# A four-layer hybrid trunk: more buffers for the local kernel blocks of the second S5 layer, and a third product buffer in the first

## The chip, the cores and the metric

The kernel runs on one core of one Trainium2 chip. The metric is the device time of one execution in microseconds (us). A lower time is better. Three executions of the kernel before were timed.

## What is computed

The reference passes 128 context tokens and 256 latent tokens (384 columns in all, 1024 features) through four residual layers: an S5 layer, a retention layer, a Hyena layer, and a second S5 layer. Only the S5 layers bear on the change. Cut to what matters:

```
u, gate = split(h @ w_in)
for d in (forward, backward):
    state[t] = A * state[t-1] + B u[t]      # 64 groups, 64 complex states each
    y       += Re(C state)
y = gelu(y)                                  # y includes d_skip * u
y = y * sigmoid(y @ w_glu + b_glu)
out = (y * silu(gate)) @ w_out
```

All data is 32-bit floating point. A dense product is made three times, with each operand split into a high part (hi) and the rest (lo).

## The kernel before, in words

The S5 scan is done in chunks of 8 tokens, 48 chunks. Within a chunk, the outputs come from a Toeplitz matrix of the local kernel. Across chunks, only the states at the chunk ends are stepped, 32 steps long, in `recur` (L771), on DVE, in two halves of 32 groups: `R0` and `R1` in the plans (L809). Each step takes a product, a shuffle and two sums (L793 to L796), and the steps of the two halves stand interleaved in DVE's order.

The stage around the change is the output stage of an S5 layer, in `s5` (L699). Channels go in 8 blocks, two at a time: four pairs, the loop over `m` (L860).

- `toeplitz(m)` (L845) loads the local kernel of block m from the scratch array `kd`: 8 transfers of 64 KB on the SP queue (L850) into one tile `Tt`. TensorE transposes it in 8 pieces into two PSUM tiles (L855), and ScalarE copies each into a half tile `Tm` (L856). `Tt` has 2 buffers, `Tm` has 7 (`TMH`). Blocks 0 to 3 are written ahead of the loop (`TMB` = 4), and block m+4 after the products of pair m (L883).
- `CP` holds the output matrices of the states, four tiles for a pair. In the second S5 layer they are loaded on the POOL queue (L867). In the first, 6 of the 16 are loaded and 10 are made by `gen_c` (L684): for each of two directions DVE writes one product into `CP` (L629) and a second product into a tile `xt` (L630), and a transfer issued by POOL adds `xt` to `CP` (L632). `xt` has 2 buffers there, and is free again when the transfer has landed.
- The products of a pair (L882) add three terms in PSUM: `Tm` by the input, and the forward and backward states by `CP`. There are 96 of them for a pair, 48 for each half r. Pairs 0 and 1 (m = 0, 2) read states of the half that R0 steps, pairs 2 and 3 (m = 4, 6) those of R1.
- Then ScalarE copies the sums (L888), TensorE transposes them (L894), and ScalarE and DVE make the GELU (L900 to L903), which also sets the PSUM tile free.

PSUM tiles of this stage (`psm`) have 4 buffers. The weight slabs `wr` (1 MB each, L153) share the SP queue with the kernel blocks, and have 2 buffers. Among them in this stage are slabs of `s5_w_in`, then four of `mod_w` (L838, read by TensorE at L379), then `s5_w_glu`. A weight is split by a cast on ScalarE (L162) and a subtraction on POOL (L134) or DVE (L149).

Each engine and each queue works in a fixed order. It is set at compile time, by a scheduler that takes, at each step of a modelled timeline, the ready instruction that comes first in the program. So the number of buffers can change orders too.

Of the kernel before, what the change touches and what calls it, by code (L numbers as in the profile page):

```python
# [10 lines left out]
F32 = mybir.dt.float32  # L11
# [34 lines left out]
BT2 = 0  # L46
TMB = 4
TMH = 7
CPB = 6
PSG = 3  # L50
GK0 = 0
# [54 lines left out]
def hybrid_trunk(ctx: ExitStack, tc: tile.TileContext, I, O, dbg=None, layers=(0, 1, 2, 3)):  # L106
    nc = tc.nc
    V, S, G, TE = nc.vector, nc.scalar, nc.gpsimd, nc.tensor
# [13 lines left out]
    def psm():  # L122
        return pm.tile([128, 512], F32, tag="m", name="psm")
# [9 lines left out]
    def gstt(out, a, b, op):  # L133
        G.tensor_tensor(out, a, b, op=op)  # L134
# [31 lines left out]
    def t384(name, bufs=5):  # L166
        return tmp.tile([128, T], F32, tag="t384", name=name, bufs=bufs)
# [6 lines left out]
    def put(parts, kb, src, sl=slice(0, T), eng=V):  # L174
        S.copy(parts[0][:, kb, sl], src)
        eng.tensor_tensor(parts[1][:, kb, sl], src, parts[0][:, kb, sl].bitcast(F32), op=OP.subtract)
# [176 lines left out]
    def tick(n=1):  # L353
        for _ in range(n):
            if bg:
                bg.popleft()()
# [279 lines left out]
    def expand_c(CP, rot, tb, xc, hb, xb, eng, add, tag="xt"):  # L636
        for d in range(2):
            expand(CP[:, d], rot, tb["B1"], tb["BI"], xc[:, d], slice(1, 9) if d == 0 else slice(8, 0, -1), d * 64 + hb * 4, xb, eng, add, tag)
# [46 lines left out]
    def gen_c(j, hb, tb, rot, CP, xb, eng=V, add=G):  # L685
        xc = rot.tile([128, 2, 2, 4, 16], F32, tag="xc", name="xc")
        nc.sync.dma_start(xc, I["s5bc"][j, hb // 4, :, hb % 4, 1])
        expand_c(CP, rot, tb, xc, hb, xb, eng, add)
# [10 lines left out]
    def s5(i, j, nxt, begun=lambda: None):  # L699
        def mk(st, name, bufs=1, **kw):  # L700
            return st.enter_context(tc.tile_pool(name=f"{name}_{i}", bufs=bufs, reuse_waits="tile", **kw))
# [9 lines left out]
        if j == 0:  # L711
# [3 lines left out]
            with ExitStack() as e2:  # L715
                tb = gen_setup(j, tpool, fpool, mk(e2, "s5p"))
# [125 lines left out]
        rot = mk(e2, "s5c", 2)  # L842
        Tms = {}

        def toeplitz(m):  # L845
            kdm = I["kd"][j * 8 + m]
            Tt = rot.tile([128, 8, 128], F32, tag="Tt", name="Tt")
            for t in range(8):
                src = bass.AP(tensor=kdm.tensor, offset=kdm.offset + (7 - t) * 16, ap=[[1920, 16], [240, 8], [1, 128]])
                nc.sync.dma_start(Tt[16 * t:16 * t + 16], src)  # L850
            for r in range(2):
                Tm = rot.tile([128, 4, 128], F32, tag="Tm", name="Tm", bufs=TMH)
                ps = psm()
                for g in range(4):
                    TE.transpose(ps[:, g * 128:(g + 1) * 128], Tt[:, r * 4 + g, :], ident)  # L855
                S.copy(Tm, ps.rearrange("p (g c) -> p g c", c=128))  # L856
                Tms[m, r] = Tm
        for m in range(TMB):
            toeplitz(m)
        for m in range(0, 8, 2):  # L860
            CP = {}
            for r, mm_ in ((r, m + q) for r in range(2) for q in range(2)):
                c = rot.tile([128, 2, 4, 8, 16], F32, tag="CP", name="CP", bufs=CPB if j == 0 else CP1)
                if j == 0 and 2 * mm_ + r not in SPL:
                    gen_c(j, 2 * mm_ + r, tb, rot, c, 2, V, None)
                else:
                    (CQ if j else nc.sync).dma_start(c.rearrange("p d g e c -> p (d g e c)"), I["cpd"][2 * mm_ + r])  # L867
                CP[mm_, r] = c
            pys = [psm(), psm()]
            Ys = rot.tile([128, 8, 8, 16], F32, tag="Ys", name="Ys", bufs=1)  # L870
            for r in range(2):
                for g in range(4):
                    gl = r * 4 + g
                    for k in range(3):
                        for q in range(2):
                            gg = (m + q) * 8 + gl
                            X = Xs[gg // XH]
                            o = pys[r][64 * q:64 * q + (48 if k else 64), g * 128:(g + 1) * 128]
                            a, b = ((U[:, m + q, gl * NCH:gl * NCH + 64], Tms[m + q, r][:, g, :]),
                                    (X[:, 0, 0:48, gg % XH], CP[m + q, r][:, 0, g].rearrange("p a b -> p (a b)")),  # L880
                                    (X[:, 1, 1:49, gg % XH], CP[m + q, r][:, 1, g].rearrange("p a b -> p (a b)")))[k]
                            TE.matmul(o, a, b, start=k == 0, stop=k == 2)  # L882
            for q in range(2):  # L883
                if m + q + TMB < 8:
                    toeplitz(m + q + TMB)
                tick(CT)
            for r in range(2):
                S.copy(Ys[:, :, r * 4:r * 4 + 4, :], pys[r].rearrange("p (g t i) -> p t g i", g=4, t=8))  # L888
            for hf in range(2):
                fb = m + hf  # L890
                o = 64 * hf
                pg = psm()
                for t in range(8):
                    TE.transpose(pg[:, t * 64:t * 64 + 48], Ys[o:o + 48, t].rearrange("p a b -> p (a b)"),  # L894
                                 ident[o:o + 48, o:o + 48])
                y = pg.rearrange("p (t c) -> p c t", t=8)[:, :48, :]
                x2 = t384("gx2").rearrange("p (c t) -> p c t", t=8)
                gf = t384("gf")
                gv = gf.rearrange("p (c t) -> p c t", t=8)
                S.activation(x2, y, AF.Square, scale=math.sqrt(0.044715))  # L900
                V.scalar_tensor_tensor(x2, x2, 1.0, y, op0=OP.add, op1=OP.mult)
                S.activation(x2, x2, AF.Tanh, scale=math.sqrt(2.0 / math.pi))
                V.scalar_tensor_tensor(gv, x2, 1.0, y, op0=OP.add, op1=OP.mult)  # L903
                put(g_parts, fb, gf)
                gstt(sgate[:, fb, :], gf, sgate[:, fb, :], OP.mult)
# [486 lines left out]
    def to3():  # L1392
        p = pool_of(e3, "x3", side="right")
        return Early(3, lambda: p.tile([128, T + 2], F32, tag="xb", name="xb", bufs=NB + EB3))
    s5(0, 0, to1)
    trace(0)
    hp = pool_of(eh, "hp")
# [5 lines left out]
    e2.close()  # L1403
    eh.close()
    s5(3, 1, lambda: None, e3.close)
    trace(3)
    rb, _ = rstd_bcast()
# [168 lines left out]
```

## Time and profile before

| | us |
|---|---|
| three timed executions | 1652.22, 1651.68, 1649.26 |
| their median | 1651.68 |
| the profiled execution, whole | 1654.23 |
| its span, first to last instruction | 1652.1 |
| TensorE busy in the span | 1460.5 |
| DVE busy in the span | 1250.0 |
| ScalarE busy in the span | 693.9 |
| POOL busy in the span | 663.5 |

The mean granted clock of TensorE in the profiled execution is 0.942 of full speed. Times of rows are us from the start of the span. The profiled execution is 2.55 us above the median of the timed ones. The first S5 layer's output stage lies at about 218 to 340 us, the second's at about 1455 to 1580 us.

A busy share says how long an engine worked. Which work sets the end is read from the chain of waits, which goes back from the last instruction to what released it at each step.

### The profile page before, as it was taken

Reading aid. Unit: us, or ns where it says so; the run is one execution under the profiler, and the core shown is the slowest. Engines: PE = TensorE matmul, PEld = TensorE weight load, DVE = VectorE, ACT = ScalarE, POOL = GpSimd, SP = SyncE. Lnnn points to the kernel's source line nnn. Section 1 sums busy time; section 2 is a strip of 40 time slices with the busy share of each in tenths; the row PEclk is TensorE's granted clock in tenths of the full one; section 3 lists DMA queues with packets and bytes.
Section 4 is the critical chain, followed back from the end, with each engine's and each line's share of the span. In section 5 each row is a group of like instructions: output and inputs, shape, how many; then the busy total and the mean of one; then the engine's idle time right before and its main releaser. Section 6 shows DMA issues by size and latency. Waiting matters only on the chain. (4 is left out here: it accounts for less than half of the span.)

```text
span 1652.1 us, 27609 instructions
## 1 busy us (share of the span) xinstructions
PE 1460.5 (88%) x10370; PEld 1290.5 (78%) x10370; DVE 1250.0 (76%) x2935; ACT 693.9 (42%) x1275; POOL 663.5 (40%) x484
## 2 busy tenths in 40 slices
PE   5878876788689999999979999999999999998796
PEld 3655664577579888889968988989999798777686
DVE  8967996589787777755868988887888863399465
ACT  2444421234324333335445545445454442642453
POOL 2111331315275756551325665556656331131221
PEclk9788897799799999999979999999999999998898
DMA  8488589743645555544333223222321353675531
GB/s 355 137 269 243 144 213 272 223 147 140 229 160 182 183 204 188 186 146 142 129 106 102 97 77 99 100 77 77 105 96 66 132 227 140 191 206 179 167 128 64
DMA packets 107805, 261.39 MB, mean 158 GB/s; under 512 B 28535, under 2 KB 68568, under 8 KB 88088
## 3 DMA queue, kind: packets, MB, share of 16 engines
q1 hardware_dynamic: 80768, 200.12, 37.0%
q0 software_dynamic: 11984, 34.87, 7.6%
q10 hardware_dynamic: 14920, 24.65, 4.1%
q8 instruction: 82, 1.34, 0.3%
q14 instruction: 51, 0.42, 0.1%
HBM read 220.37 MB, written 30.83 MB: 152 GB/s over the span
## 5 line engine op out<-in xcount | busy, mean ns | idle before, releaser
L134 POOL TENSOR_TENSOR wl<-wr,wh 128x1024 fp32r<-128x1024 f32 (+2 forms) x99 | 249.7, 2524 | 313.3 <-ACT wh L162 286.2
L162 ACT CAST wh<-wr 128x1024 fp32r<-128x1024 f32 (+4 forms) x211 | 216.0, 1029 | 314.7 <-PE psd L139 222.3
L139 PE MATMUL psd<-hh,wh 128*128 128x384 f32 x880 | 305.0, 348 | 13.8 <-DVE X L796 5.1
L139 PE MATMUL psd<-hh,wl 128*128 128x384 f32 x880 | 303.4, 345 | 5.4 <-POOL wl L134 3.4
L139 PE MATMUL psd<-hl,wh 128*128 128x384 f32 x880 | 303.9, 345 | 2.7 <-DVE hl L470 2.5
L149 DVE TENSOR_TENSOR wl<-wr,wh 128x1024 fp32r<-128x1024 f32 (+3 forms) x112 | 146.7, 1311 | 72.8 <-ACT wh L162 70.3
L139 PEld LDWEIGHTS psd<-hh,wh 128*128 128x128 f32 x880 | 168.2, 192 | 26.2 <-issue 14.3
L139 PEld LDWEIGHTS psd<-hh,wl 128*128 128x128 f32 x880 | 168.3, 191 | 13.8 <-issue 5.1
L139 PEld LDWEIGHTS psd<-hl,wh 128*128 128x128 f32 x880 | 168.3, 191 | 12.4 <-issue 6.4
L139 PE MATMUL psd<-wh,hh 128*128 128x256 f32 x384 | 111.1, 293 | 3.9 <-ACT k L1075 1.8
L139 PE MATMUL psd<-wl,hh 128*128 128x256 f32 x384 | 110.7, 290 | 4.1 <-DVE wl L149 2.2
L139 PE MATMUL psd<-wh,hl 128*128 128x256 f32 x384 | 109.2, 286 | 0.0
L379 PE MATMUL psn<-wr,sgc 128*32 128x256 f32 x640 | 57.0, 449 | 30.7 <-DMA wr<-in_mod_w_dram 25.5
L630 DVE TENSOR_TENSOR xt<-BI,xc 128x512 f32<-128x512 f32 x52 | 47.2, 911 | 44.9 <-DMA CP<-xt 18.9
L139 PE MATMUL psd<-zb,wh 128*128 128x384 f32 x240 | 80.9, 338 | 0.0
L139 PEld LDWEIGHTS psd<-wl,hh 128*128 128x128 f32 x384 | 74.4, 194 | 6.2 <-DVE wl L149 3.1
L139 PEld LDWEIGHTS psd<-wh,hh 128*128 128x128 f32 x384 | 74.0, 194 | 6.1 <-ACT k L1075 2.3
L634 POOL TENSOR_TENSOR BP<-BP,xt 128x512 f32<-128x512 f32 x32 | 46.7, 1460 | 69.8 <-DVE xt L630 47.8
L139 PEld LDWEIGHTS psd<-wh,hl 128*128 128x128 f32 x384 | 74.4, 194 | 0.1
L630 DVE TENSOR_TENSOR xt<-FI,bc 128x512 f32<-128x512 f32 x64 | 51.8, 809 | 17.8 <-POOL BP L634 9.8
L632 POOL DMA_DIRECT2D CP<-xt x32 | 28.0, 929 | 92.7 <-DVE xt L630 43.6
L634 POOL TENSOR_TENSOR CP<-CP,xt 128x512 f32<-128x512 f32 x32 | 50.1, 1565 | 31.1 <-DVE xt L630 19.5
(385 smaller groups left out, 3890.4 us busy)
## 6 DMA issues: line engine op xcount, KB each, us to landing
wr<-in_mod_w_dram SPq DMA_DIRECT2D x40, 1024.0 KB
wr<-in_hy_w_in_dram SPq DMA_DIRECT2D x32, 1024.0 KB
wr<-in_ret_w_in_dram SPq DMA_DIRECT2D x24, 1024.0 KB
wr<-in_s_w_in_dram SPq DMA_DIRECT2D x16, 1024.0 KB
wm<-in_mod_w_dram SPq DMA_DIRECT2D x8, 1024.0 KB
CP<-xt POOLq DMA_DIRECT2D x32, 256.0 KB, 6.9
Tt<-scratch_kd_dram SPq DMA_DIRECT2D x128, 64.0 KB
wr<-in_s_w_glu_dram SPq DMA_DIRECT2D x8, 1024.0 KB
```

Of the source, the lines that this page charges most:

```text
L134: G.tensor_tensor(out, a, b, op=op)
L139: TE.matmul(out, lhs[a], rhs[b], start=start and i == 0, stop=stop and i == len(combos) - 1)
L149: V.tensor_sub(out, a, b)
L162: S.copy(hi, ap)
L379: TE.matmul(ps[q * 32:(q + 1) * 32, :256], sg[:, kb, 6 - 2 * u:38 - 2 * u], raw[:, kb, :], start=u == 0 and k2 == 0, stop=u == 3 and k2 == 1)
L630: eng.tensor_tensor(t, c2, x[:, 1].unsqueeze(2).to_broadcast([128, 4, 8, 16]), op=OP.mult)
L632: nc.gpsimd.dma_start(out, t, accum_op=OP.add)
L634: add.tensor_tensor(out, out, t, op=OP.add)
```

## The change

In the second S5 layer (j = 1) `Tt` gets four buffers in place of two, and `Tm` eight half tiles in place of seven. The number of blocks that are written ahead of the loop stays four. In the output stage of the first S5 layer (j = 0), where `gen_c` makes the output matrices, `xt` gets three buffers in place of two. No instruction is added or removed.

```diff
+TT1 = 4
+TM1 = 8
...
-            Tt = rot.tile([128, 8, 128], F32, tag="Tt", name="Tt")
+            Tt = rot.tile([128, 8, 128], F32, tag="Tt", name="Tt", bufs=2 if j == 0 else TT1)
...
-                Tm = rot.tile([128, 4, 128], F32, tag="Tm", name="Tm", bufs=TMH)
+                Tm = rot.tile([128, 4, 128], F32, tag="Tm", name="Tm", bufs=TMH if j == 0 else TM1)
...
-                    gen_c(j, 2 * mm_ + r, tb, rot, c, 2, V, None)
+                    gen_c(j, 2 * mm_ + r, tb, rot, c, 3, V, None)
```

## Rows read from the trace of the kernel before

**Rows 1.** The page's chain that ended last: share of the span by line

```profile
PE psd L139 5%; PE psm L882 1%; DVE sw L794 1%; DMA Tt<-scratch_kd_dram 1%; DVE X L795 1%; DVE X L796 1%; DVE m L793 1%; PE psm L747 0%; SPq L850 0%; DVE wl L149 0%; DVE sgate L532 0%; PE psm L756 0%; PE psm L855 0%; ACT wh L162 0%; DVE xT L1415 0%
```

**Rows 2.** The chain in order of time, second output stage: start, us, what

```profile
1528.71 10.38 DMA Tt<-scratch_kd_dram
...
1543.01 6.49 DMA Tt<-scratch_kd_dram
...
1553.16 7.00 PE psm L882 x96
...
1563.37 5.39 PE psm L882 x96
```

**Rows 3.** TensorE's timeline, second output stage: start, us, instruction, idle before

```profile
1476.93 1.04 PE L855 MATMUL psm<-ident,Tt 128*128 128x128 f32 x8
...
1518.30 0.68 PE L882 MATMUL psm<-CP,X 128*48 128x128 f32 x8 [2.84 <-DVE X L796]
...
1524.07 1.07 PE L379 MATMUL psn<-wr,sgc 128*32 128x256 f32 x16
...
1543.06 1.94 PE L855 MATMUL psm<-ident,Tt 128*128 128x128 f32 x8 [4.03 <-DMA Tt<-scratch_kd_dram]
...
1549.74 1.94 PE L855 MATMUL psm<-ident,Tt 128*128 128x128 f32 x8 [4.73 <-DMA Tt<-scratch_kd_dram]
```

**Rows 4.** The SP queue's timeline, second output stage

```profile
1455.95 16.28 SPq L850 DMA_DIRECT2D Tt<-scratch_kd_dram  x16
...
1513.89 0.52 SPq L153 DMA_DIRECT2D wr<-in_mod_w_dram  x1
1514.46 7.87 SPq L850 DMA_DIRECT2D Tt<-scratch_kd_dram  x5
1522.43 3.10 SPq L153 DMA_DIRECT2D wr<-in_s_w_glu_dram  x2
1526.81 16.79 SPq L850 DMA_DIRECT2D Tt<-scratch_kd_dram  x16
```

**Rows 5.** Two stretches: busy us of PE, PEld, DVE, ACT, POOL; clock; DMA share; GB/s

```profile
1500.00:1518.00 18.00, 15.45 (x121) 12.00 (x119) 18.00 (x122) 3.01 (x5) 2.51 (x1) 1.00 0.57 190
...
1538.00:1553.00 15.00, 6.24 (x38) 5.24 (x37) 0.02 (x1) 2.03 (x4) 0.94 (x2) 0.66 0.68 168
```

**Rows 6.** DVE's timeline: the weight's lo part within R1, and R1's last step

```profile
1528.63 0.82 DVE L149 TENSOR_TENSOR wl<-wr,wh 128x640 fp32r<-128x640 f32 x1 [2.14 <-PE psm L894]
...
1537.80 0.23 DVE L796 TENSOR_TENSOR X<-X,sw 128x64 f32<-128x64 f32 x1
```

**Rows 7.** ScalarE's timeline: half tiles that wait for a free buffer, a cast

```profile
1521.96 1.07 ACT L856 COPY Tm<-psm 128x512 f32<-128x512 f32 x2 [5.44 <-PE psm L882]
...
1527.87 1.35 ACT L162 CAST wh<-wr 128x640 fp32r<-128x640 f32 x2 [1.02 <-DMA wr<-in_s_w_glu_dram]
```

**Rows 8.** POOL's timeline, and (last line) landing times of the CP tiles, second layer

```profile
1533.52 1.12 POOL L867 DMA_DIRECT2D CP<-scratch_cpd_dram  x2
...
DMA to landing us min/median/max: 4.0/8.3/11.8
```

**Rows 9.** DVE's timeline, first output stage

```profile
291.55 1.29 DVE L630 TENSOR_TENSOR xt<-BI,xc 128x512 f32<-128x512 f32 x2
303.67 0.69 DVE L630 TENSOR_TENSOR xt<-BI,xc 128x512 f32<-128x512 f32 x1 [10.84 <-DMA CP<-xt]
...
310.91 0.69 DVE L630 TENSOR_TENSOR xt<-BI,xc 128x512 f32<-128x512 f32 x1 [4.83 <-DMA CP<-xt]
311.51 0.55 DVE L903 SCALAR_TENSOR_TENSOR gf<-gx,psm 128x384 f32<-128x384 f32 x1
```

**Rows 10.** TensorE's timeline, first output stage: pair 2, second half

```profile
312.21 0.70 PE L882 MATMUL psm<-Tm,U 128*64 128x128 f32 x4 [7.34 <-DVE gf L903]
```

**Rows 11.** POOL's timeline, and (last line) landing times of the sums, first layer

```profile
292.54 1.75 POOL L632 DMA_DIRECT2D CP<-xt  x2 [4.73 <-DVE xt L630]
...
DMA to landing us min/median/max: 3.3/6.3/11.5
```

## The prediction

> **What bounds the kernel now.** I read the page's chain first, by line, to see where the end is decided [rows 1]. Most of it is dense products and DVE's state steps, but 1% of the span is the landing of kernel blocks, `Tt<-scratch_kd_dram`. The chain in order of time puts that into one place [rows 2]: one landing of 10.38 us and one of 6.49 us, both just ahead of pair 2 of the second S5 layer's output stage. TensorE's timeline shows the same from the other side [rows 3]: it stands still for 4.03 us before the transposes of block 6 and for 4.73 us before those of block 7, and pair 2's products begin behind both, at 1553.16 [rows 2]. The SP queue's timeline says why [rows 4]: the last 16 pieces, blocks 6 and 7, are issued from 1526.81 on, behind two 1 MB slabs. With two `Tt` buffers, blocks 6 and 7 wait for the transposes of blocks 4 and 5, which run only about when pair 0 ends. Nothing else asks for that delay: the state half that pairs 2 and 3 read is complete at 1537.80 + 0.23 = 1538.0 [rows 6]. In the stretch of the two stalls DVE works 0.02 of 15 us and TensorE's granted clock is 0.66 [rows 5]. The first S5 layer has a stop of another kind, below.
>
> **The change, part by part. Second layer, four Tt buffers.** The 64 pieces and 64 transposes stay as many; only their places move. The first 16 issues take 16.28 us, 1.02 us each [rows 4]. Blocks 0 to 3 need no transpose any more, blocks 4 to 7 only those of blocks 0 to 3. At 1.02 us each, 64 issues from 1455.95 on end at about 1521, where they now end at 1526.81 + 16.79 = 1543.6. Even with 10 us of waits for weight slabs in between, block 7 lands (6.49 after its issue) before TensorE asks for it at 1543.06 - 4.03 = 1539.0. The bytes have room: from 1500 to 1518 the DMA engines are busy only 0.57 of the time [rows 5].
>
> What that takes off the path:
> - the two stalls, 4.03 + 4.73 = 8.8 us [rows 3];
> - the slow clock behind them: 8 transposes take 1.94 us there and 1.04 us at the granted clock of 1.00 [rows 3], twice 0.9 = 1.8 us; pair 2's 96 products take 7.00 us where pair 3's take 5.39 [rows 2], 1.6 us.
>
> Together 12.2 us, which is the upper bound. Pair 2 would begin at 1553.1 - 8.8 - 1.8 = 1542.5. What is late next? R1's end at 1538.0 is not. The last two `CP` tiles of pair 2 are issued at 1533.52 and land after 8.3 us (median), 11.8 at most [rows 8], so at 1541.8 to 1545.3; the second half of the pair needs them at about 1545.2. So they just hold. The copies of the half tiles (0.54 us each, half of a 1.07 us row of two [rows 7]) stand between transposes and products. I leave 1.2 us for them and take 11 us. The lower bound is 0: the stalls stay if the blocks do not come earlier.
>
> **Eight half tiles.** With seven, the second half of block 3 waits for the first half of pair 0's products, and ScalarE stands 5.44 us at it [rows 7]. With eight that copy goes early; but then a half of block 4 waits in the same place. TensorE waits for R0's last state until 1518.30 anyway [rows 3], so I cost it at 0; without that cover it would be worth at most the 5.44 us. The larger pool also shifts where `CP` lies; its first tiles are not read before 1518.30, so 0 as well.
>
> **First layer, third xt buffer.** DVE makes two second products at 291.55, and the next waits 10.84 us for a free `xt`; one more waits 4.83 us at 310.91 [rows 9]. The cause is the sums' landing: issued at 292.54, the first sets its tile free at 303.67, 11.1 us later, where the median is 6.3 [rows 11]. Behind these waits on DVE stands a GELU step, at 311.51 [rows 9], and it holds the PSUM tile for which TensorE stops 7.34 us before pair 2's second half, at 312.21 [rows 10]. With a third buffer the product at 303.67 is made at once, the one after it takes its place at 303.67, and the one at 310.91 goes at about 305, when the second sum has landed. The GELU step then comes at about 306, 5.4 us earlier. Pair 2's second half also needs the sum issued from 304 now; it would be issued at about 294.3 and land by 305.8 with the longest landing of 11.5 [rows 11]. So 5 us. Upper bound: both waits, 15.7 us. Lower bound: a loss of 2.8 us, four second products of 0.69 us [rows 9] put ahead of state steps. I take 5, as the next landing bounds it.
>
> Sum: 11 + 5 = 16 us. The profiled execution, 1654.2, would become 1638.2; against the median of 1651.7, 2.55 below it, it is **1635.7**, say 1636. About 0.2% (3.3 us) is what a measurement of this kernel can tell from no change.
>
> **The rivals.**
>
> *The first layer gives nothing.* Orders are set by a model in which a sum may land sooner than the 6 to 11 us of the chip, so DVE may just put another second product ahead of the GELU and wait again. For it: two such products stand ahead of it now. Time 1651.7 - 11 = 1640.7.
>
> *The GLU's slab comes late.* Pulling 16 pieces (1 MB) ahead of it moves the 1 MB slab of 1522.43 back. Its cast now comes at 1527.87, already 1.02 us late [rows 7], and DVE, in the middle of R1, stands 2.14 us at 1528.63 for the part made from it [rows 6] (the row names TensorE; the cast ended just then). At 190 GB/s, the rate of 1500 to 1518 [rows 5], 1 MB takes 5.5 us. ScalarE's copies and R1 would both be 5 to 6 us later, R1's end 1543.4, and the 11 us would become 6: 1640.7. Against it: at 1.02 us each all pieces are issued by 1521, so the slab's issue at 1522.43 need not move. The Trainium skill, "DMA: Bandwidth & Descriptors", section "Queues, rings and completion order", has the rule behind this: SP's transfers share one ring on each DMA engine, and descriptors are consumed in ring order. The trace agrees: pieces issued behind two slabs take 10.38 us to land, later ones 6.49 [rows 2]. By the rule alone, whatever is gained for the blocks is paid by the slab, and the sum would be 1640.7 rather than 1635.7.
>
> *The blocks do not come earlier.* If the new order puts them behind slabs that wait for a buffer, the stalls stay: only the first layer's 5 us, 1646.7. If neither part acts, 1651.7.
>
> *Slower: a mod_w slab behind the blocks.* TensorE's order has the last group of `mod_w` products inside pair 0, at 1524.07 [rows 3]; its slab is issued at 1513.89 [rows 4]. If blocks 6 and 7 go ahead of it, 16 issues at the 1.57 us that five of them took next to slabs (7.87 us [rows 4]) are 25 us: the products come at 1549, and pairs 0, 1 and 2 shift by 25. Pair 2 begins at 1542.5 + 25 = 1567.7, 14.6 us later than now; less the first layer's 5, 1661. It decides from a delay of some 16 us, 10 pieces. Against it: that slab stands earlier in the program than the blocks, so it goes first whenever its buffer is free.
>
> **How the numbers follow.** Chances: the forecast 0.50; nothing from the first layer 0.17; the slab late 0.15; blocks not earlier 0.05; neither part 0.05; slower 0.08. The range 1629 to 1648: its low end takes both upper parts (12.2, and 10 of the first layer's 15.7), its high end takes in the blocks that do not come earlier, and 0.13 and some tails stay out. The first four cases are faster by over 0.2%; with a tail of each taken off for orders that shift elsewhere, faster 0.83, same 0.07, slower 0.10.
>
> **What the profile of the changed kernel would show.** Right: the last block issue on SP before about 1530; no TensorE wait for `Tt` ahead of pair 2; pair 2's first product some 10 us earlier against R1's last step; clock near 1.00 there. DVE's 10.84 us wait for `xt` gone, and pair 2's second half of the first layer 5 us earlier. Wrong: a wait of TensorE for `Tt` or `CP` of over 3 us ahead of pair 2, a `mod_w` wait inside pair 0, DVE standing at the GLU slab's lo part for over 5 us, or a GELU step of the first layer still behind a wait for `xt`.

## The result and the profile after

The changed kernel took 1633.4 us (median of four runs, 1632.3 to 1636.9), the kernel before 1651.1 on the same count: ratio 0.9886, 95% interval 0.9866 to 0.9907. That is 17.7 us less where 16 were predicted, and 1633.4 lies in the range of 1629 to 1648. Two later measurements of the same kernel, beside the experiments below, gave 0.9866 (0.9829 to 0.9904) and 0.9882 (0.9856 to 0.9909), 22 and 19 to 20 us. The three together say some 20, a little more than predicted. The profiled execution of after took 1632.3 us (span 1630.5, clock 0.951), so the two profiled ones stand 21.6 us apart in span. Line numbers of after are two higher than those of before.

**Second layer.** The chain by line of the changed kernel has no landing of a block in it; in its place stands the first GLU slab. It answers to [rows 1].

```profile
PE psd L141 5%; PE psm L884 1%; DVE X L797 1%; DVE m L795 1%; PE psm L749 1%; DVE sw L796 1%; DMA wr<-in_s_w_glu_dram 1%; DVE X L798 1%; PE psm L758 0%; ACT wh L164 0%; ACT X L761 0%; PE psm L857 0%; DVE sgate L534 0%; DVE wl L151 0%; PE psn L381 0%
```

The chain in order of time, in the second output stage (start, us, what), answers to [rows 2]:

```profile
1506.69 1.11 PE psm L857 x4
1507.81 1.87 PE psn L381 x16
1509.67 4.08 PE psm L884 x66
...
1515.03 9.21 DMA wr<-in_s_w_glu_dram
...
1526.51 0.48 ACT Ys L890
...
1533.18 5.39 PE psm L884 x96
...
1541.78 5.39 PE psm L884 x96
```

Pair 2 now takes 5.39 us, as long as pair 3, where it took 7.00. It starts at 1533.11 where it started at 1553.16, 20.0 us earlier; the stage itself starts 10.6 us earlier (first block issue at 1445.38 instead of 1455.95), so 9.4 us were gained inside the stage. With the 1.6 us of the faster clock that is 11.0. The SP queue's timeline shows why, against [rows 4]:

```profile
1445.38 12.35 SPq L852 DMA_DIRECT2D Tt<-scratch_kd_dram  x16
...
1464.35 17.83 SPq L852 DMA_DIRECT2D Tt<-scratch_kd_dram  x14
...
1504.18 10.75 SPq L852 DMA_DIRECT2D Tt<-scratch_kd_dram  x10
1515.03 45.07 SPq L155 DMA_DIRECT2D wr<-in_s_w_glu_dram  x4
```

The last block piece is issued by 1514.93, 69.6 us after the first. All 64 now stand ahead of the GLU slabs; before, 16 stood behind two of them. TensorE's timeline of the stage, against [rows 3], and the row of 1524 to 1540 from the view by windows (columns as in [rows 5]):

```profile
1506.69 1.11 PE L857 MATMUL psm<-ident,Tt 128*128 128x128 f32 x4 [3.63 <-ACT Tm L858]
...
1509.60 0.87 PE L884 MATMUL psm<-CP,X 128*48 128x128 f32 x8
...
1527.03 1.02 PE L857 MATMUL psm<-ident,Tt 128*128 128x128 f32 x4 [2.55 <-ACT Ys L890]
...
1533.11 0.44 PE L884 MATMUL psm<-Tm,U 128*64 128x128 f32 x4
```

```profile
1524.00:1540.00 16.00, 13.45 (x149) 12.63 (x148) 8.73 (x20) 9.78 (x19) 5.27 (x7) 0.89 0.67 253
```

The two waits for `Tt`, 8.8 us together, are gone, and the granted clock ahead of and in pair 2 is 0.89, where it was 0.66 ahead of pair 2. Two shorter waits are new: 3.63 us ahead of pair 0, in place of the 2.84 us for R0's state [rows 3], and 2.55 us ahead of block 7's transposes. The second comes from ScalarE, as ScalarE's timeline shows (against [rows 7]), and DVE's shows the rest (against [rows 6]):

```profile
1512.04 1.07 ACT L858 COPY Tm<-psm 128x512 f32<-128x512 f32 x2 [5.40 <-PE psm L884]
...
1524.32 1.35 ACT L164 CAST wh<-wr 128x640 fp32r<-128x640 f32 x2 [4.07 <-DMA wr<-in_s_w_glu_dram]
...
1526.41 0.56 ACT L890 COPY Ys<-psm 128x512 f32<-128x512 f32 x1
```

```profile
1525.08 0.83 DVE L151 TENSOR_TENSOR wl<-wr,wh 128x640 fp32r<-128x640 f32 x1 [3.20 <-ACT wh L164]
...
1529.54 0.21 DVE L798 TENSOR_TENSOR X<-X,sw 128x64 f32<-128x64 f32 x1
```

The slab is the rival that came half true. Issued behind ten pieces, it lands 9.2 us after its issue, where the cast began 5.4 us after it before [rows 4, 7]. ScalarE stands 4.07 us at the cast, with the copy of `Ys` behind it, and TensorE loses 2.55. DVE stands 3.20 us in R1 (2.14 before). But R1's last step ends at 1529.75, 3.4 us ahead of pair 2, so that costs nothing more. The price on TensorE is 2.55 us here and not 5. It differs from run to run: in the two later profiles of the same kernel ScalarE stands 3.47 and 1.44 us at this cast and TensorE 1.96 us and not at all. The row of the last of them, from ScalarE's timeline:

```profile
1518.25 1.35 ACT L164 CAST wh<-wr 128x640 fp32r<-128x640 f32 x2 [1.44 <-DMA wr<-in_s_w_glu_dram]
```

The Trainium skill, "DMA: Bandwidth & Descriptors", section "Queues, rings and completion order", says that descriptors are consumed in ring order. The trace agrees in kind, since the slab behind ten pieces lands 9.2 us after its issue.

**First layer.** DVE's waits from 235 to 345 us (total, times, longest) come to 18.9 us for a landed sum before and to 2.4 after; the wait for `xc` is now the longest (against [rows 9]). First before, then after:

```profile
DVE xt L630 <- DMA CP<-xt: 18.9, 5, 10.8
```

```profile
DVE CP L631 <- DMA xc<-in_s5bc_dram: 10.3, 3, 4.6
DVE gx L903 <- ACT gx L902: 3.6, 3, 1.9
DVE xt L632 <- DMA CP<-xt: 2.4, 3, 1.8
```

TensorE's timeline of after, in pair 2's second half, at its last transposes and pair 3's last products (against [rows 10]), and POOL's, with the last sums (against [rows 11]):

```profile
307.66 0.45 PE L884 MATMUL psm<-CP,X 128*48 128x128 f32 x1
...
315.79 0.99 PE L896 MATMUL psm<-ident,Ys 48*128 48x48 f32 x16
...
321.57 0.61 PE L884 MATMUL psm<-CP,X 128*48 128x128 f32 x8
```

```profile
310.03 1.75 POOL L634 DMA_DIRECT2D CP<-xt  x2 [5.51 <-DVE xt L632]
```

By the span's clock the bulk of pair 2's second half, its last 38 products, begins at 307.66 where the half began at 312.21: 4.6 us, close to the predicted 5. But that is chance, since the whole stage lies later in this profile. The SP queue's first block issue, in before and then in after:

```profile
182.50 5.82 SPq L850 DMA_DIRECT2D Tt<-scratch_kd_dram  x8
```

```profile
189.26 5.69 SPq L852 DMA_DIRECT2D Tt<-scratch_kd_dram  x8
```

In the two later profiles of the changed kernel the stage begins at 183.22 and 183.26, so a shift of this size lies between runs of one program, and nothing shows it to be the change's. Counted from that issue, pair 2's second half begins at 129.7 us in before, and its last 38 products at 118.4, 117.6 and 118.2 in the three profiles of the changed kernel: some 11 us, where the prediction had 5. Pair 3's last product ends at 132.9 (by the span's clock 322.2), where it ended at 151.5 (334.0): 18.6 us. DVE's timeline of after shows what became of the GELU step:

```profile
293.31 0.55 DVE L905 SCALAR_TENSOR_TENSOR gf<-gx,psm 128x384 f32<-128x384 f32 x1
...
298.06 0.68 DVE L632 TENSOR_TENSOR xt<-BI,xc 128x512 f32<-128x512 f32 x1
```

Pair 1's two GELU steps (293.31 and 296.08) now stand ahead of pair 2's last second product (298.06). From the stage's first issue they come at 104 and 107 us, where the one that held TensorE came at 129. The rest of before's TensorE and POOL timelines, which the prediction did not read, says where some 7 of the 18.6 us come from:

```profile
322.14 0.44 PE L882 MATMUL psm<-Tm,U 128*64 128x128 f32 x4
...
325.03 0.38 PE L882 MATMUL psm<-CP,X 128*48 128x128 f32 x2
...
330.21 0.47 PE L882 MATMUL psm<-CP,X 128*48 128x128 f32 x4 [0.25 <-DMA CP<-xt]
...
331.58 0.35 PE L882 MATMUL psm<-CP,X 128*48 128x128 f32 x1 [0.36 <-DMA CP<-xt]
```

```profile
322.53 1.77 POOL L632 DMA_DIRECT2D CP<-xt  x2 [1.08 <-PE psm L894]
```

In before, pair 3's own last sums were issued at 322.53, behind the same blocked second products on DVE, and landed at 330 to 331.5. Pair 3's second half was torn in two by that; dense products filled the gap, so the wait is written as 0.25 and 0.36 us and does not look like one. In after those sums go at 310.03 (120.8 us after the stage's first issue, where it was 140.0) and pair 3 runs through.

### The profile page after: what moved, and what is told of

Read it like the earlier page. It is cut to its first block, busy times and chain, and to the rows that moved or that the text cites. A ratio compares the mean times of both kernels' runs of the same rounds, so it can differ in the third digit from the quotient of the medians.

```text
span 1630.5 us, 27608 instructions
## 1 busy us (share of the span) xinstructions
PE 1449.2 (89%) x10370; PEld 1280.7 (79%) x10370; DVE 1246.0 (76%) x2935; ACT 692.2 (42%) x1275; POOL 664.3 (41%) x484
## 5 line engine op out<-in xcount | busy, mean ns | idle before, releaser
L631 DVE TENSOR_TENSOR CP<-B,xc 128x512 f32<-128x512 f32 x52 | 52.9, 1044 | 26.5 <-DMA scratch_cpd_dram<-CP 15.6
L381 PEld LDWEIGHTS psn<-wr,sgc 128*32 128x32 f32 x640 | 20.0, 124 | 56.9 <-DMA wr<-in_mod_w_dram 27.8
L797 DVE TENSOR_TENSOR X<-X,m 128x64 f32<-128x64 f32 x184 | 64.2, 349 | 0.0
## 6 DMA issues: line engine op xcount, KB each, us to landing
CP<-xt POOLq DMA_DIRECT2D x32, 256.0 KB, 7.2
```

Of the source, the lines that this page charges most:

```text
L381: TE.matmul(ps[q * 32:(q + 1) * 32, :256], sg[:, kb, 6 - 2 * u:38 - 2 * u], raw[:, kb, :], start=u == 0 and k2 == 0, stop=u == 3 and k2 == 1)
L631: eng.tensor_tensor(out, c1, x[:, 0].unsqueeze(2).to_broadcast([128, 4, 8, 16]), op=OP.mult)
L797: V.tensor_add(dst, dst, m1[:, 0])
```

## The experiments

Twelve more runs were made in three groups of four, each group on a chip of its own, each run timed beside the kernel before. The groups are: changed_again, blocks_only, xt3_only, seven_halves; pair2_dve, pair3_dve, pool_sums, glu_pool; changed_third, both_dve, three_tt, seven_glu. Runs of one and the same program spread over up to 16 us (1626 to 1642), so the table also has each profiled execution cut into stretches. A: from the first output stage's first block issue to the start of its last product. B: from the span's start to the retention layer's first instruction on DVE, a shuffle. C: from where the SP queue is released for the second output stage's first block (some 0.15 us ahead of that issue) to the end of the span. All in us, from the traces. A and C are quieter than the total. B is not, as the first output stage begins anywhere from 182.5 to 192.2 us.

| kernel | ratio to before (95%) | A | B | C |
|---|---|---|---|---|
| before | 1 | 151.2 | 456.6 | 196.3 |
| changed, first profile | 0.9886 (0.9866 to 0.9907) | 132.6 | 445.2 | 185.3 |
| changed_again | 0.9866 (0.9829 to 0.9904) | 134.8 | 443.3 | 184.0 |
| changed_third | 0.9882 (0.9856 to 0.9909) | 132.7 | 439.2 | 182.7 |
| blocks_only | 0.9920 (0.9890 to 0.9951) | 148.8 | 456.6 | 182.2 |
| xt3_only | 0.9928 (0.9903 to 0.9952) | 132.6 | 443.0 | 193.5 |
| seven_halves | 0.9870 (0.9842 to 0.9897) | 133.5 | 446.0 | 184.8 |
| pair2_dve | 0.9936 (0.9912 to 0.9960) | 142.8 | 449.8 | 188.1 |
| pair3_dve | 0.9946 (0.9923 to 0.9970) | 142.4 | 459.8 | 187.8 |
| both_dve | 0.9939 (0.9914 to 0.9963) | 134.2 | 451.1 | 188.0 |
| pool_sums | 0.9889 (0.9855 to 0.9923) | 128.0 | 447.8 | 185.0 |
| glu_pool | 0.9855 (0.9827 to 0.9884) | 132.9 | 447.5 | 182.5 |
| three_tt | 0.9871 (0.9838 to 0.9904) | 136.5 | 454.0 | 181.0 |
| seven_glu | 0.9885 (0.9853 to 0.9917) | 132.8 | 445.5 | 180.4 |

**The changed kernel again**, without an edit, as the base for the runs beside it.

> The changed kernel once more, on the same chip as the three kernels beside it. It should be about 17 to 18 us below the kernel before (1651 to 1633.5), the difference of the medians shown so far. If it is nearer to 22, the two profiled executions, and not the medians, give the size.

> The changed kernel a third time, as the base for the three kernels beside it on the same chip: 18 to 22 us below the kernel before, by the two measurements so far (ratios 0.9886 and 0.9866).

0.9866 and 0.9882, the second as in the first measurement (0.9886), the first some 3 us better; the mean of the three, 0.9878, is 20 us.

**The two parts, each alone.**

```diff
 # blocks_only
-                    gen_c(j, 2 * mm_ + r, tb, rot, c, 3, V, None)
+                    gen_c(j, 2 * mm_ + r, tb, rot, c, 2, V, None)
 # xt3_only
-TT1 = 4
-TM1 = 8
+TT1 = 2
+TM1 = 7
```

> Only the second layer's part: four Tt and eight Tm buffers there, two xt buffers in the first layer as before. By the prediction -11 us (about 1640); the profiles say the same, since between the start of the second layer's output stage and the start of pair 2's products the changed kernel gains 9.4 us more than before it, and 1.6 more by the end. The rival, that the blocks gain nothing by themselves and all of the gain is the first layer's, gives 1651; the rival that a late GLU slab takes half back gives 1645.

> Only the third xt buffer of the first layer; Tt two and Tm seven in the second layer as before. By the prediction -5 us (1646). By the profiles of the two kernels the first layer and the retention layer after it stand 8.3 us earlier, and the second S5 stage 10.6 earlier, so the trace's theory says -7 to -8 (1643.5). The two parts should add up to the changed kernel's gain within 2 us if they don't act on each other.

Before had a median of 1655.2 beside these; so blocks_only is worth 13.2 us (8.1 to 18.2) and xt3_only 11.9 (7.9 to 16.1). The 11 of the prediction lies inside the first interval, its 5 outside the second, and the 7 to 8 that I read from the two profiles just at its edge. The sum, 25.1, is 2.9 above the 22.2 of the changed kernel beside them, a little beyond the 2 expected but within the intervals. TensorE's waits show that each part acts in its own place. First the longest of blocks_only from 1480 to 1575 us, then one of its rows from 235 to 340, then the longest of xt3_only from 1480 to 1575:

```profile
PE psm L857 <- ACT Tm L858: 4.8, 1, 4.8
```

```profile
PE psm L884 <- DVE gf L905: 8.5, 2, 7.4
```

```profile
PE psm L857 <- DMA Tt<-scratch_kd_dram: 9.0, 2, 4.9
```

With the blocks alone the two waits for `Tt` are gone and the first layer's wait for the GELU step stays; with the third buffer alone it is the other way round. C falls by 11.4 us (mean of before and xt3_only 194.9, of the three changed profiles and blocks_only 183.6); the three kernels with DVE's sums, below, keep only 7 of it (188).

**Seven half tiles** (`TM1 = 7` in the changed kernel).

> The changed kernel with seven half tiles Tm in the second layer in place of eight. By the prediction the eighth is worth nothing (within 2 us of the changed kernel, about 1633.5): it only lets ScalarE's copies of the fourth block run ahead of pair 0. If it matters, the copies behind pair 0's products make TensorE stand before pair 0 or 1, up to the 5.4 us by which the prediction bounded it (1639).

0.9870, and C of 184.8: nothing to tell from eight. TensorE's waits from 1490 to 1560 us say what the eighth moves:

```profile
PE psm L884 <- DVE X L798: 5.0, 1, 5.0
```

With seven, TensorE waits for the state itself ahead of pair 0, whose products begin 3.2 us behind R0's last `XF` step (1510.67 to 1507.50). With eight it has block 4's transposes first, waits 3.63 us there, and pair 0 begins 4.8 us behind that step (1509.60 to 1504.77; 4.8 us too in changed_again and changed_third). The eighth loses 1.6 us here; the total shows nothing of it.

**Which wait of the first layer pays.** Two xt buffers again, but the sums of one pair added by DVE, which ends the wait for landings in that pair.

```diff
 # pair2_dve (pair3_dve: m == 6; both_dve: m > 2)
-                    gen_c(j, 2 * mm_ + r, tb, rot, c, 3, V, None)
+                    gen_c(j, 2 * mm_ + r, tb, rot, c, 2, V, V if m == 4 else None)
```

> The changed kernel with two xt buffers in the first layer again, but the four sums of pair 2 added by DVE (0.69 us each) in place of accumulating transfers, so that no landing stands in pair 2. Measured against blocks_only (1642.0 where the kernel before was 1655.2 and the changed kernel 1630.4, so the third buffer is worth 11.6 there). The prediction's theory, that the third buffer acts by pair 2's second half alone: the whole gain comes back, less the DVE time, 1630 to 1633. The trace's theory, two gains, 6.4 us in front of pair 2's second half and the rest where pair 3 no longer waits for its own late sums (0.25 and 0.36 us of wait with dense products in between, its last product 7.3 us earlier than a shift by 6.4 explains): about 1636. In the profile TensorE's 7.3 us wait for the GELU step should be gone and pair 3's waits for CP still there.

> The same with DVE's additions in pair 3 alone, pair 2's sums by transfers with two buffers. The prediction's theory: nothing, 1642. The trace's theory: TensorE's 7.3 us wait in front of pair 2's second half stays, pair 3's second half follows its first at once, and 3 to 5 us come back: 1637 to 1639.

> The changed kernel with two xt buffers in the first layer, and the sums of pairs 2 and 3 (eight of them) added by DVE, so that neither pair waits for a landing. Each alone gave nothing that could be told from blocks_only. The theory that the two waits stand in series, and that what is freed at one is lost at the other: together they bring back what the third buffer brings, 10 to 12 us below blocks_only, within 3 us of the changed kernel; in the profile pair 2's second half to pair 3's last product takes about 14.5 us, where it takes 21.8 in the kernel before. The rival, that the third buffer acts through the other order that it sets from the start of the first output stage: nothing comes back, 9 to 12 us above the changed kernel.

TensorE's timeline of pair2_dve, pair 3's products before and after the gap, then DVE's; and last TensorE's wait from 235 to 345 us in pair3_dve:

```profile
314.74 0.38 PE L884 MATMUL psm<-CP,X 128*48 128x128 f32 x2
319.48 0.47 PE L884 MATMUL psm<-CP,X 128*48 128x128 f32 x4
324.80 0.35 PE L884 MATMUL psm<-CP,X 128*48 128x128 f32 x1
```

```profile
308.73 0.69 DVE L632 TENSOR_TENSOR xt<-BI,xc 128x512 f32<-128x512 f32 x1 [1.21 <-DMA CP<-xt]
...
315.61 0.69 DVE L632 TENSOR_TENSOR xt<-BI,xc 128x512 f32<-128x512 f32 x1 [5.05 <-DMA CP<-xt]
```

```profile
PE psm L884 <- DVE gf L905: 8.4, 2, 7.7
```

Pair2_dve has no wait for the GELU step any more, but pair 3 is still torn (314.74, 319.48, 324.80), behind a second product that waits 5.05 us for its tile. Pair3_dve keeps the wait of 7.7 us for the GELU step, and pair 3 stops for only 0.41. The times missed: by their ratios none of the three is faster than blocks_only, and both_dve is 9 us above the changed kernel, as its rival had it. In stretch A, though, the theory stands: from 150.0 (mean of before and blocks_only) pair 2 alone takes off 7.2, pair 3 alone 7.6, both 15.8, and the third buffer 15 to 17 in seven of eight profiles with the sums left to the transfers. So the two waits are two gains of like size that add up; they are not in series, as I had supposed. The other order that the rival names is there as well: counted from the stage's first issue, pair 1 ends after 91 to 97 us in the eight profiles with the third buffer and sums by transfers, and after 111 to 115 in the five with two buffers. But both_dve, with pair 1 late, ends pair 2 after 119.5 us and has a stretch A of 134.2, as those eight do (120.0 to 126.7 us, 132.6 to 136.5), so within the stage that order is not what pays. What both_dve then loses lies elsewhere: from ScalarE's last GLU tanh (its start at 366.8, against 368.1 in the changed kernel) to the retention layer's first shuffle it takes 84.3 us, where the changed kernel takes 77.1 and before 80.3, and its C is 4 us longer, with a wait of TensorE of 5.3 us for `sgate` where changed_third has 1.3. An edit in one stage changes the order that is set in later ones: in the second output stage the block pieces go in groups of 16, 18, 14, 3, 7 and 6 in these three kernels, and of 16, 14, 14, 2, 8 and 10 in the changed kernel. That these orders cost the rest was read from the stretches; it wasn't tried by itself.

**All sums on POOL.**

```diff
-                    gen_c(j, 2 * mm_ + r, tb, rot, c, 3, V, None)
+                    gen_c(j, 2 * mm_ + r, tb, rot, c, 3, V, G)
```

> The changed kernel with all sums of the first layer's output stage made by POOL's adder in place of accumulating transfers (about 1.3 us each by POOL's 1.0 us for a tile of three quarters the size), three buffers. If what the third buffer buys is only freedom from the landing of 6 to 11 us, this is at least as good as the changed kernel, within 2 us or up to 3 better, since 2.4 us of DVE's waits for a landing are left there. The rival: POOL's adds slow DVE down or come late in POOL's order, and it is 2 to 5 us slower than the changed kernel.

0.9889; the changed kernel, which was not timed on that chip, has 0.9866 to 0.9886, and the intervals overlap: no gain, and the rival's 2 to 5 us neither shown nor excluded. A is the shortest of all, 128.0, but the 5 us that it gains do not arrive: from the stage's first issue to the retention layer it takes 259.2 us, the changed kernel 256.0 to 260.1. DVE's timeline and then POOL's show one price of it:

```profile
268.86 4.66 DVE L631 TENSOR_TENSOR CP<-B,xc 128x512 f32<-128x512 f32 x4
```

```profile
269.69 4.96 POOL L636 TENSOR_TENSOR CP<-CP,xt 128x512 f32<-128x512 f32 x3 [11.09 <-DVE CP L631]
...
275.42 1.28 POOL L636 TENSOR_TENSOR CP<-CP,xt 128x512 f32<-128x512 f32 x1 [0.77 <-DVE xt L632]
```

Side by side, four of DVE's products take 1.17 us each, where one takes 0.69 by itself, and three of POOL's sums 1.65, where one takes 1.28. That this is all of what is lost was not shown.

**The GLU slab on POOL's queue.**

```diff
 # weight() takes a queue; dense_late:
-        raws = [weight(wsrc[s]) for s in range((n + 1) // 2)]
+        raws = [weight(wsrc[s], nc.gpsimd) for s in range((n + 1) // 2)]
```

> The changed kernel with the second layer's first two GLU slabs issued on POOL's queue in place of SP's, so that they don't stand behind the last ten block pieces. The theory that the slab is what is late next: ScalarE's 4.07 us wait for it and TensorE's 2.55 us wait before block 7's transposes go, and the time falls by 2 to 4 us against the changed kernel. The rival, that the transfers share the same engines and the slab or a block is as late on another queue: no change, or up to 4 us more where a block comes late.

The waits from 1440 to 1560 us, TensorE's longest and then ScalarE's for the slab:

```profile
PE psm L857 <- ACT Tm L858: 4.8, 1, 4.8
...
ACT wh L164 <- DMA wr<-in_s_w_glu_dram: 1.7, 1, 1.7
```

ScalarE's wait is 1.7 us where after's profile has 4.1, and TensorE's 2.55 us ahead of block 7 is gone; the one ahead of pair 0, for a half tile, is as long as in the other kernels with eight. But changed_third, without this edit, has 1.4 us, no wait of TensorE for the copy of `Ys`, and a C of 182.7 where this one has 182.5. So the waits do not show that the queue did it. The ratio, 0.9855, against 0.9866 to 0.9886 for the changed kernel on other chips, cannot tell 2 us from none: inconclusive, in time and as a wait.

**Three Tt buffers** (`TT1 = 3`).

> The changed kernel with three Tt buffers in the second layer in place of four. Only block 7 then waits for a transpose that runs near pair 0 (block 4's, about 1507 in the changed kernel), and its eight pieces are issued by about 1517. The theory that the gain comes from the pieces leaving before the GLU slabs, not from four blocks standing ready: within 2 us of the changed kernel, no wait of TensorE for Tt ahead of pair 2. The rival, that the last block comes late again: one stall of some 4.7 us comes back, 3 to 5 us slower.

0.9871 against 0.9882, C of 181.0, and no wait of TensorE for `Tt` in the stage. Three do what four do: with either, all pieces leave ahead of the slabs. Two were one short.

**Seven halves and the slab on POOL's queue together.**

> The changed kernel with seven half tiles and the first two GLU slabs on POOL's queue. By the profiles each saves a little: with seven, pair 0 begins 3.2 us behind R0's last XF step where with eight it begins 4.8 behind; with the slab on POOL's queue TensorE's 2 to 2.6 us wait before block 7's transposes is gone. If they add, 3 to 4 us below the changed kernel, the best so far. If R1 or the CP tiles of pair 2 then decide when pair 2 begins, 0 to 1 us.

0.9885 against 0.9882: no gain that could be measured, though C, 180.4, is the shortest. No version measurably beat the changed kernel.

## Why the prediction came out

- **Four Tt buffers, 11 us: right.** Blocks_only and the stretch C give 11 to 13. The two stalls (8.8) and the slow pair 2 (1.6) went as worked out. The signs named ahead came: all block issues done before 1530 (1514.93), no wait for `Tt` ahead of pair 2, its first product 3.4 us behind R1's end where it was 15.1. Only the clock is 0.89 in that stretch and not 1.00; TensorE still waits 2.55 us in it.
- **Eight half tiles, 0: right.** As the prediction put it, a half of block 4 now waits in the same place, 5.40 us against 5.44 [rows 7].
- **Third xt buffer, 5 us: right in mechanism, too small in size.** The failed step is "I take 5, as the next landing bounds it". It kept DVE's order, with the GELU step behind a second product at about 305, and it took the longest landing, 11.5 us. With three buffers the GELU steps stand ahead of pair 2's last second product (298.06), and the sum made from that, issued at 299.03, lands after 7.4 us. So pair 2's second half begins some 11 us earlier in its stage and not 5. The term then took this shift for the shift of all that follows, but pair 3's own last sums hung on the same two buffers and went 19.3 us earlier in the stage (12.5 by the span's clock). In stretch A the third buffer is worth 16.4 us, just above the bound of 15.7 made of both waits. B falls by 11.1 us (456.6 in before and blocks_only, 445.5 as the mean of the eight kernels with the buffer in its place). The stage begins 3.9 us later in these eight, within the spread of one program (183.2 to 189.3); counted from its first issue, 15.0 us arrive at the retention layer.
- **The rivals.** "The first layer gives nothing" and "the blocks do not come earlier" are excluded by xt3_only and blocks_only. "The GLU's slab comes late" is there, at half its price or less (2.55, 1.96 and 0 us on TensorE in three profiles). A `mod_w` slab behind the blocks did not happen: the last one is issued at 1503.60, ahead of the last ten pieces.
- **The sum.** 16 predicted, 17.7 measured at first, about 20 by all three measurements: the first layer's term is the difference. That the total came so near is in part luck: this term was under half of the 11.9 us that xt3_only measured, and the first measurement is the lowest of the three (18.8, 22.2 and 19.5 us by their ratios).

## What to carry to other kernels

Where a buffer is short, follow every later group that uses it to the end of the stage before putting a price on one more, not only the first wait that it clears. A torn group whose gap other work fills hides its loss from the list of waits; look at the group's first and last instruction. And where a planner sets the order, judge an edit by stretches: totals mix its own effect with new orders elsewhere. Count a stretch from its own first instruction, because the same program reached this stage 6 us later in one profile than in two others.

## What the runs showed that I had not expected

- DVE's products and POOL's sums slow each other when they run side by side: from 0.69 to 1.17 us and from 1.28 to 1.65 us, above. The Trainium skill, "SBUF — State Buffer", section "Who interferes with whom", says that a DVE instruction with two SBUF inputs contends with a GpSimd instruction that reads SBUF; the trace agrees.
- In pair 2's second half of the first layer the granted clock is 0.82 where it was 0.52 (nearly all of it at the lower level, 1.2 GHz). Before, TensorE stood still for 7.34 us ahead of it, and now its last 38 products come straight from 16 `mod_w` products behind a wait of 1.83; they take 2.8 us, where all 48 took 5.4. The prediction had counted this effect in the second layer and not in the first. The rows by windows, before and then after (columns as in [rows 5]):

```profile
312.20:317.60 5.40, 5.35 (x48) 4.97 (x48) 4.71 (x8) 2.92 (x6) 3.73 (x4) 0.52 1.01 354
```

```profile
307.60:310.50 2.90, 2.90 (x42) 2.62 (x38) 2.50 (x5) 0.00 (x0) 0.47 (x1) 0.82 1.06 321
```

- Three_tt's profiled execution took 1642.1 us, where the median of its runs is 1628.4. Most of that lies in the first layer, and more than half of it ahead of the output stage: B is 454.0, 14.8 us above changed_third's, and the stage's first block is issued at 192.21 against 183.26. Within the stage A is 3.8 us longer, and TensorE waits 15.8 us for `mod_w` slabs from 235 to 345 us, 12.8 in changed_third. What makes the stage begin later in some runs was not followed further.
